# Planned lengths of matrix products, and VectorE planned apart from GpSimd, in a kernel that plans its own queues

## The chip, the cores and the metric

The kernel runs on one core of a Trainium2 chip. The metric is the device time of one execution in microseconds (us). TensorE is called PE here, VectorE DVE, ScalarE ACT, GpSimd POOL and SyncE SP, as in the profile. The clock that TensorE is granted has two levels, 1.2 and 2.4 GHz.

## The reference

Two transformer blocks work on 512 tokens of 1024 features, in float32. The first has a convolution layer and a layer of forgetting attention, each with a feed-forward network and a gated projection of a side input. The second has three branches that are gated and summed, and a gated feed-forward network. Cut to what matters here:

```python
# first block, layer 0 then layer 1
h = h + conformer_conv(rmsnorm(h), ...)         # layer 1: h + fox_attention(...), 16 heads of 64
h = h + square(relu(rmsnorm(h) @ ffn_w1)) @ ffn_w2
h = h + sigmoid(rmsnorm(h) @ ple_w_gate) * (p @ ple_w_proj)
# second block
xa, ga, qm, km, vm, qx, g_logits = split(rms_norm(x) @ w_in)
y_a = rg_lru(causal_dwconv(xa), ...) * gelu(ga)     # gated linear recurrence
y_b = moba_attention(qm, km, vm)                    # 8 heads of 64
y_c = memory_cross_attention(qx, mem_k, mem_v)      # 4 heads of 128
x = x + sum(sigmoid(g_logits) * branch_out(y_a, y_b, y_c)) @ w_out
x = x + (gelu(causal_dwconv(h @ w_gate)) * (h @ w_up)) @ w_down
```

## The kernel before

Activations lie feature-major: a tile holds 128 features by 512 tokens. A product of float32 accuracy is made of three products of float32r halves: weights come as panels of 2048 columns, and each panel is split into `hi` (a cast by ACT) and `lo` (a subtraction by DVE or POOL), each input into `xh` and `xl`; `mm3` issues hi times xh, hi times xl and lo times xh. Most of the program is such groups of 24 products of 512 columns into one bank of PSUM.

Beside this stream run side jobs: the splits of the next panels, the splits of new activations, norms, and the attention heads. A head takes four blocks of 128 queries; for each, PE makes scores (`sc`), DVE the maximum, ACT the exponential `P` (which frees the bank of the scores, of which there are two), POOL scales `P` by the reciprocal, PE transposes it (`ptp`), ACT and DVE split the transposed block (`pth`, `ptl`), and at the end of a head PE multiplies with the values.

No scheduler of a compiler sets the order. The kernel writes instructions in the order in which its own planner reaches them, and each engine runs its own in that order. Every operation goes through `Engine` (line 73): it issues the instruction and asks a cost function (lines 98 to 121) how long it will take. `Flow.account` (line 144) sets the end of the operation on a planned clock: not before the engine's previous one, and not before its inputs. After each operation of PE the planned time moves on and `poll` starts each side job that is then due. `quiet` tells a side job to go on when the named engines are planned to be free. So a duration in a cost function decides how many products stand in the queue of PE before the next step of a side job, and in what order the queues of ACT, DVE and POOL are filled. Nothing is timed at run time: waits are on semaphores.

The planned length of a float32r product is set at line 121:

```python
    return max(0.109 if dt == F32R else 0.059, n / 2390)
```

Three places matter below. In the recurrence of the second block (from line 1328), ACT makes the gelu of four tiles `ga`, after which each is multiplied by the recurrence's output and split (`ya`):

```python
        for f in range(4):
            act.activation(ga[f], ga[f], AF.Gelu_apprx_tanh)
            yield flow.quiet(act)
        for f in range(4):
            yield [ga[f], xc[f]]
            dve.tensor_mul(ga[f], ga[f], xc[f])
            yield ga[f]
            ya[f] = split(ga[f])
```

`branch` (line 1442) multiplies two gate panels (`gl`) with the input and then a panel `br` with `ya`; its first product needs `ya[0]`. The heads of the block attention run beside it. The second place is the end of the forgetting attention (from line 1236): the output panels `("o", 1, 0)` and `("o", 1, 1)` take the last heads' results as they come. The third is a norm (`Front.chain`, line 495): the sum of squares of the last tile goes to PE (`tp<-C,sq`), through DVE and POOL, and back to PE (`tp<-C,s`), beside the 48 products of the first panel of the next stage.

Of the kernel before, what the change touches and what calls it, by code (L numbers as in the profile page):

```python
# [8 lines left out]
F32 = mybir.dt.float32  # L9
F32R = mybir.dt.float32r  # L10
# [5 lines left out]
S = 512  # L16
# [8 lines left out]

# [1 line left out]
_VECS = [  # L27
# [45 lines left out]
class Engine:  # L73
    """an engine whose instructions are issued in the order of the trace, with an estimate of when each one ends"""

    def __init__(self, flow, eng, cost):
        self.flow, self.eng, self.cost, self.t, self.table = flow, eng, cost, 0.0, None

# [36 lines left out]
def _pe_cost(op, out, ins):  # L115
    n, dt = ins[1].free_size(), ins[1].dtype
    if op == "transpose" or (dt == F32 and n == 1):
        return 0.11
    if dt == F32:
        return 0.01 + n * 4 / 2400  # L120
    return max(0.109 if dt == F32R else 0.059, n / 2390)


class Flow:
    """Weaves side work into the stream of matrix products. Every engine issues in the order of this trace; a side is
    a generator that yields what its next step waits for: a time (us), tiles, or a condition."""

# [16 lines left out]
    def account(self, eng, outs, ins, cost):  # L144
        ko = [k for a in outs for k in self.spans(a)]
        ki = [k for a in ins for k in self.spans(a)]
        at = eng.t
        for k in ki + ko:
            at = max(at, self.ready.get(k, 0.0) - (WRITE if k in ko else 0.0))
        for k in ko:  # L150
            at = max(at, self.used.get(k, 0.0))
        eng.t = at + cost
        for k in ki:
            self.used[k] = max(self.used.get(k, 0.0), eng.t)
        for k in ko:
            self.ready[k], self.used[k] = eng.t + WRITE, eng.t
        if eng is self.pe:
            self.now = eng.t
            self.poll()
# [67 lines left out]
def kernel(ctx: ExitStack, tc, gain0, x_t, p_t, mem_t, vec, w, w_f, w_lru, rows, consts, out):  # L227
# [9 lines left out]
    flow = Flow()  # L237
    act, dve = Engine(flow, nc.scalar, _act_cost), Engine(flow, nc.vector, _dve_cost)
    pool, pe = Engine(flow, nc.gpsimd, _pool_cost), Engine(flow, nc.tensor, _pe_cost)
    flow.pe = pe  # L240

# [39 lines left out]

# [1 line left out]
    V = cp.tile([128, NV], F32, name="V")  # L283
# [11 lines left out]

# [1 line left out]
    raws, parts = {}, {}  # L297
# [9 lines left out]
    def part(i, k, pieces, low):  # L307
        """piece k of a panel's split, its low part on engine low"""
        if k == 0:
            parts[i] = tuple(wp.tile([128, PW], F32R, name=nm(n), tag=n, bufs=2) for n in ("hi", "lo"))  # L310
        r, (hi, lo), c = raws[i], parts[i], PW // pieces
        s = slice(c * k, c * k + c)
        gain = GAINED.get(_KEYS[i][0])
        if gain is not None:
            g = col(gain, k)
            act.activation(hi[:, s], r[:, s], AF.Copy, scale=g)
            dve.scalar_tensor_tensor(lo[:, s], r[:, s], g, hi[:, s].bitcast(F32), op0=ALU.mult, op1=ALU.subtract)
        else:
            act.copy(hi[:, s], r[:, s])
            low.tensor_sub(lo[:, s], r[:, s], hi[:, s].bitcast(F32))  # L320
# [40 lines left out]
    def gemm(ps, pan, c0, xs, width=256, ks=None, m=128):  # L361
        """ps += panel columns (from c0 of each k tile)^T x; ks: the k tiles of this call"""
        hi, lo = pan
# [7 lines left out]
    def couter(pan, xs, ks=None, banks=None):  # L371
        """both output tiles of a panel, k tile by k tile"""
        banks = banks or [bank(), bank()]
        for k in range(len(xs)) if ks is None else ks:
            for j in range(2):
                gemm(banks[j], pan, 128 * j, xs, ks=[k])
        return banks

    def pairs(keys, xs):
        """output tiles of the panels in turn; the first panel k tile by k tile, while x still comes"""  # L380
        for i, key in enumerate(keys):
# [9 lines left out]

# [1 line left out]
    def split(src, g=None, n=S, scale=None):  # L393
        """exact two-part float32r split of src * g (g per feature)"""
        xh, xl = slot(F32R, "xh"), slot(F32R, "xl")
# [8 lines left out]
    def split_into(dst, k, src, g=None):  # L404
        """the same in steps, into dst[k]"""
        n = src.shape[-1]
# [12 lines left out]
    class Norm:  # L419
        """per-token mean over features of squares"""  # L420

# [48 lines left out]
    class Front:  # L470
        """input of a stage: gained splits of the stream's tiles as they come, and the norm's factor"""

# [36 lines left out]

# [1 line left out]
    G0 = cp.tile([128, KT], F32, name="G0")  # L511
# [32 lines left out]
    def diagonals(fs):  # L544
        """diagonal matrices of the last PE_TAPS[f] taps of a tile, both parts"""
        for f in fs:
# [27 lines left out]
    def conv_dve(order):  # L574
        """two tiles at a time, tap by tap in turn, so that none waits for its own sum; sums in PSUM"""
        todo, active = list(order), []
# [112 lines left out]

    # products that wait for nothing of the stream: ple projections, memory keys and values  # L690
    prd = dp.tile([KT, 128, S], F32, name="prd")

    def gemm32(ps, raw, c0, xs, width, m=128):
        """float32 products as they are, for panels whose splitting would hold other engines up"""
        n = len(xs)
# [64 lines left out]

    # layer norm over features, two passes
    ys = [None] * KT
# [56 lines left out]

# [1 line left out]
    def squared(z, k, t):  # L821
# [37 lines left out]

# [1 line left out]
    def diag(t, i):  # L861
        """query block i of transposed probabilities: key block j, query block i lies at column 384 j + 128 i"""
        a = t[:, 128 * i:128 * i + 128]
        return bass.AP(tensor=a.tensor, offset=a.offset, ap=[a.ap[0], [384, i + 1], [1, 128]])

    class Head:
        """causal attention of the head in rows 64 half.. of kt() and qt(); out() [128, S] takes a pair of heads"""

# [137 lines left out]
        def weigh(self):  # L1006
            """out[64 rows] = values^T probabilities^T; [V_hi | V_lo] or [V_lo | V_hi]"""
            vs = self.vs()
# [22 lines left out]
    class MemHead(Head):  # L1031
        """attention of one head of 128 features to the memory"""

# [48 lines left out]
    def attend(heads, period, gap):  # L1082
        """scores head by head, at least a period apart; all that follows as its inputs come"""
        state = {"scored": 0}
# [17 lines left out]
    def values(key, xs, r4):  # L1102
        """token-major values of 4 heads, split: per key block [128, 512]"""
        pan = panel(key)
        vs = []
        for b in range(4):
            ps = bank()
            token_major(ps, pan, xs, b)
            t = slot(F32R, "v")
            # heads 0,2: [hi|lo]; heads 1,3: [lo|hi]  # L1110
            v5 = t.rearrange("p (a b c d) -> p a b c d", a=2, b=2, c=2)
# [8 lines left out]

# [1 line left out]
    # the stream's tiles go in as they are, the gains into the weights; h is the sum of the two parts again  # L1122
    xs = front.xs
# [141 lines left out]

# [1 line left out]
    gg = small(8, "gg")  # L1267
# [47 lines left out]

    # gated linear recurrence
    xa, ga = [None] * 4, [None] * 4
# [10 lines left out]
    def recurrence():  # L1328
        # -8 softplus(-lam)
        lam = V[:, _VOFF["lam"]:_VOFF["lam"] + 4]  # L1330
# [53 lines left out]
        for f in range(4):  # L1384
# [4 lines left out]
            yield q  # L1389
            # 1 - a^2 = -tanh(log a) (1 + a^2)  # L1390
            dve.scalar_tensor_tensor(th[f], q, 1.0, th[f], op0=ALU.add, op1=ALU.mult)
# [24 lines left out]

    # block attention: of two blocks of 256 keys the past one is always chosen, so every earlier key counts
    rw, rr_ = slot(p="rows"), slot(F32R, "rowsr")
# [65 lines left out]

    # memory cross attention
    qx = [None] * 4
# [22 lines left out]

    # gated feed forward with a causal convolution on the gate  # L1510
    norms = [Norm(HALF) for _ in range(2)]
# [35 lines left out]

    # the last two panels token half by token half: the first one's norm and output go beside the second's products
    pre = [slot(p="out") for _ in range(2)]
# [67 lines left out]

# [1 line left out]
def _pack(inp):  # L1619
# [3 lines left out]
    def wide(m, c0, n):  # L1623
        """columns c0..c0+n of m [K, N] as [128, K/128 * n]"""
        k = m.shape[0] // 128
# [96 lines left out]

    # shapes alone: identity, causal mask, 1/1024, distance rows
    consts = np.zeros((128, 257), np.float32)
# [41 lines left out]
```

## Time and profile before

| what | value |
|---|---|
| time, median of 3 runs | 2154.78 us (2154.36 to 2157.05) |
| the profiled execution: span, first to last instruction | 2154.4 us (the page gives no other time of its own) |
| PE busy with products | 2109.2 us, 98% of the span, 9920 instructions |
| DVE, ACT, POOL busy | 1270.6, 937.4, 370.5 us |
| mean granted clock of TensorE | 0.993 of 2.4 GHz |
| moved by DMA | 204.79 MB, 95 GB/s on average |

The busy share of PE counts from each product's start to its modelled end, and consecutive products overlap; the pitch from start to start says more than the mean duration. What the table can't say is where PE stands still, and for whom: that is read from the waits, engine by engine, and from the timeline around each.

### The profile page before, as it was taken

What the parts mean: (1) busy time and instruction counts of PE and PEld (TensorE: products, weight loads), DVE (VectorE), ACT (ScalarE), POOL (GpSimd) and SP (SyncE); (2) the same over time, 40 slices, a digit from 0 to 9 for tenths busy, and PEclk for the clock granted to TensorE, in tenths of its full rate; (3) what the DMA queues carried; (4) which work ended last, traced back from release to release, by engine and by line L of the source; (5) the groups of instructions that cost most, each with busy time, mean ns of one, the idle gap of its engine ahead of it and who ended that gap; (6) DMA issues with size and microseconds to landing.
All of it is one profiled execution on the core that took longest, in us unless ns stands there. A gap on an engine that the chain in (4) does not pass through costs nothing. (4 is left out here: it accounts for less than half of the span.)

```text
span 2154.4 us, 26102 instructions
## 1 busy us (share of the span) xinstructions
PE 2109.2 (98%) x9920; PEld 1741.6 (81%) x9920; DVE 1270.6 (59%) x2166; ACT 937.4 (44%) x1884; POOL 370.5 (17%) x380
## 2 busy tenths in 40 slices
PE   7999999999999999999999999999999999999998
PEld 6867888888878887788888887778888888888887
DVE  5997534344576887544343567775564556465563
ACT  5766423233446676433232453665452333232222
POOL 5881100000121336300000031331010010000002
PEclk9999999999999999999999999999999999999999
DMA  5215232232222111222222233112222422222221
GB/s 183 98 45 190 86 110 80 97 104 92 98 80 85 61 61 60 79 98 98 98 93 89 95 125 129 71 64 95 98 79 79 142 93 98 100 96 98 95 101 59
DMA packets 38444, 204.79 MB, mean 95 GB/s; under 512 B 4648, under 2 KB 7976, under 8 KB 15920
## 3 DMA queue, kind: packets, MB, share of 16 engines
q1 hardware_dynamic: 37744, 202.62, 26.8%
q8 instruction: 78, 1.28, 0.2%
q10 hardware_dynamic: 576, 0.52, 0.1%
q14 instruction: 46, 0.38, 0.1%
HBM read 195.45 MB, written 7.68 MB: 94 GB/s over the span
## 5 line engine op out<-in xcount | busy, mean ns | idle before, releaser
L83 PE MATMUL mm<-xh,hi 128*128 128x512 f32 (+1 forms) x2544 | 991.5, 390 | 9.3 <-ACT hi L83 8.4
L83 PE MATMUL mm<-xl,hi 128*128 128x512 f32 (+1 forms) x2544 | 990.5, 389 | 0.0
L83 PE MATMUL mm<-xh,lo 128*128 128x512 f32 (+1 forms) x2544 | 990.0, 389 | 0.2
L83 PEld LDWEIGHTS mm<-xh,hi 128*128 128x128 f32 x2544 | 480.2, 189 | 105.0 <-ACT hi L83 8.4
L83 PEld LDWEIGHTS mm<-xh,lo 128*128 128x128 f32 x2544 | 480.1, 189 | 96.5 <-DVE lo L83 1.5
L83 PEld LDWEIGHTS mm<-xl,hi 128*128 128x128 f32 x2544 | 480.2, 189 | 94.3
L83 ACT CAST hi<-raw 128x512 fp32r<-128x512 f32 x636 | 354.3, 616 | 288.6 <-PE mm L83 268.9
L83 DVE TENSOR_TENSOR lo<-raw,hi 128x512 fp32r<-128x512 f32 x584 | 387.9, 713 | 50.3 <-ACT hi L83 48.8
L83 POOL TENSOR_TENSOR sq<-sq,sq 128x512 f32<-128x512 f32 (+1 forms) x69 | 84.7, 1230 | 1330.0 <-ACT sq L83 1329.4
L83 DVE TENSOR_TENSOR h<-mm,h 128x512 f32<-128x512 f32 (+1 forms) x113 | 75.6, 671 | 279.7 <-PE mm L83 279.6
L83 ACT ACTIVATE z<-z 128x512 f32<-128x512 f32 x64 | 40.4, 631 | 205.3 <-DVE z L83 205.3
L83 DVE SCALAR_TENSOR_TENSOR z<-mm,rbc 128x512 f32<-128x512 f32 x64 | 44.0, 690 | 120.7 <-PE mm L83 120.7
L83 POOL TENSOR_SCALAR P<-P,s 128x128 f32<-128x128 f32 (+2 forms) x112 | 65.3, 588 | 243.6 <-DVE s L83 151.0
L83 DVE TENSOR_TENSOR t<-mm,rbc 128x512 f32<-128x512 f32 x80 | 54.9, 688 | 82.5 <-PE mm L83 78.7
L83 DVE TENSOR_TENSOR xl<-z,xh 128x512 fp32r<-128x512 f32 x64 | 44.3, 693 | 74.7 <-ACT xh L83 74.7
L83 ACT ACTIVATE t<-t 128x512 f32<-128x512 f32 x40 | 25.2, 631 | 128.5 <-DVE t L83 128.4
L83 POOL TENSOR_TENSOR acc<-acc,tap 128x482 f32<-128x482 f32 (+29 forms) x60 | 77.3, 1288 | 13.1 <-ACT tap L83 9.5
L83 DVE SCALAR_TENSOR_TENSOR sc<-u,V,sc 128x511 f32<-128x511 f32 (+21 forms) x116 | 78.9, 732 | 0.5
L83 ACT ACTIVATE xh<-h,V 128x512 fp32r<-128x512 f32 x40 | 28.6, 722 | 112.4 <-DVE h L83 112.4
L83 POOL TENSOR_TENSOR lo<-raw,hi 128x512 fp32r<-128x512 f32 x52 | 69.6, 1363 | 38.8 <-ACT hi L83 38.6
L83 ACT CAST pth<-ptp 128x128 fp32r<-128x128 f32 (+2 forms) x112 | 46.1, 418 | 53.2 <-PE ptp L83 52.6
L83 ACT ACTIVATE P<-sc,s 128x128 f32<-128x128 f32 (+2 forms) x112 | 58.5, 524 | 18.1 <-DVE s L83 17.4
(228 smaller groups left out, 2235.8 us busy)
## 6 DMA issues: line engine op xcount, KB each, us to landing
raw<-in_w SPq DMA_DIRECT2D x175, 1024.0 KB
h<-in_x_t SPq DMA_DIRECT2D x8, 256.0 KB
prd<-pr SPq DMA_DIRECT2D x8, 256.0 KB
pr<-prd SPq DMA_DIRECT2D x8, 256.0 KB
resid<-h SPq DMA_DIRECT2D x8, 256.0 KB
h<-resid SPq DMA_DIRECT2D x8, 256.0 KB
out<-out SPq DMA_DIRECT2D x12, 128.0 KB
raw<-in_w SPq DMA_DIRECT2D x4, 256.0 KB
```

Source lines behind the costliest of these rows:

```text
L83: f(out, *args, **kw)
```

## The change

It alters the planner alone; the computation, its tiles and its pools stay. The planned length of a float32r product of n columns becomes 0.0133 + n/2400 us and at least 0.11 (for 512 columns 0.2267 in place of 0.2142), that of a float32 product at least 0.25 (with one column 0.25 in place of 0.11). DVE operations with two inputs in SBUF of at least 64 elements, and POOL operations with one such input, are planned one after the other: each keeps in `lock` when it ends, and the other engine's next such operation starts no earlier. The costs of ACT, DVE and POOL are as before. The docstrings and comments that the diff also drops are left out here.

```diff
@@ class Engine
-        self.flow, self.eng, self.cost, self.t, self.table = flow, eng, cost, 0.0, None
+        self.flow, self.eng, self.cost, self.t, self.table, self.lock = flow, eng, cost, 0.0, None, 0.0
@@ def _pe_cost(op, out, ins):
     n, dt = ins[1].free_size(), ins[1].dtype
-    if op == "transpose" or (dt == F32 and n == 1):
+    if op == "transpose":
         return 0.11
     if dt == F32:
-        return 0.01 + n * 4 / 2400
-    return max(0.109 if dt == F32R else 0.059, n / 2390)
+        return max(0.25, 0.01 + n * 4 / 2400)
+    return max(0.11, 0.0133 + n / 2400) if dt == F32R else max(0.059, n / 2390)
@@ def account(self, eng, outs, ins, cost):
         at = eng.t
+        other = {self.dve: self.pool, self.pool: self.dve}.get(eng)
+        locks = other is not None and sum(
+            a.space != bass.MemoryType.PSUM and a.free_size() >= 64 for a in ins) >= (2 if eng is self.dve else 1)
+        if locks:
+            at = max(at, other.lock)
...
         eng.t = at + cost
+        if locks:
+            eng.lock = eng.t
@@ def tile_two_blocks_kernel
-    flow.pe = pe
+    flow.pe, flow.dve, flow.pool = pe, dve, pool
```

The queues come out in another order almost everywhere: the operations are the same ones, but for ACT_TABLE_LOAD, which ACT's queue holds 23 times before and 29 times now.

The first place is ACT's queue in the second block, where the four gelus stand (`ga`; `P` is an exponential of an attention block, `hi` a cast of a weight panel). Before:

```order
L83 ACT_TABLE_LOAD
L83 ACTIVATE ga1822_10866<-ga1822_10866 128x512
L83 ACTIVATE ga1823_10868<-ga1823_10868 128x512
L83 ACTIVATE ga1837_10932<-ga1837_10932 128x512
L83 ACTIVATE ga1851_10995<-ga1851_10995 128x512
L83 CAST hi1890_11278<-raw1870_11148 128x512
L83 ACT_TABLE_LOAD
L83 ACTIVATE P1904_11355,s1905_11356<-sc1893_11298,s1898_11317 128x128
L83 ACTIVATE P1906_11363,s1907_11364<-sc1899_11320,s1900_11330 128x256
L83 CAST xh1908_11368<-ga1822_10866 128x512
```

The same place in ACT's queue now, from the third gelu to the fourth (the first two stand 29 and 17 rows earlier):

```order
L83 ACT_TABLE_LOAD
L83 ACTIVATE ga1835_10928<-ga1835_10928 128x512
L83 ACT_TABLE_LOAD
L83 ACTIVATE P1965_11566,s1966_11567<-sc1951_11523,s1952_11530 128x512
L83 CAST pth1960_11552<-ptp1967_11569 128x2x128
L83 COPY t1969_11582<-mm1968_11572 64x512
L83 ACTIVATE P1973_11593,s1974_11594<-sc1962_11556,s1964_11564 128x128
L83 ACT_TABLE_LOAD
L83 ACTIVATE ga1846_10980<-ga1846_10980 128x512
L83 CAST pth1960_11552<-ptp1977_11604 128x3x128
L83 ACT_TABLE_LOAD
```

The four gelus stood in a row behind one table load, ahead of the first exponential; now exponentials stand between them, each change of function loads a table, and the split of `ya[0]` (`xh1994`, a CAST from ga1822) comes seven rows behind the last gelu.

The same place in PE's queue: the last products of the second tile of the first gate panel, and the first product of panel `br`, which takes `ya[0]`. Before:

```order
L83 MATMUL mm1936_11455<-xh1775_10572,hi1890_11278 128x512
L83 MATMUL mm1936_11455<-xl1776_10573,hi1890_11278 128x512
L83 MATMUL mm1936_11455<-xh1775_10572,lo1891_11279 128x512
L83 MATMUL mm1949_11516<-xh1908_11368,hi1922_11416 128x512
L83 MATMUL mm1949_11516<-xl1909_11369,hi1922_11416 128x512
```

Now the last product of the gate panel is followed by side work; these are the first rows of it:

```order
L83 MATMUL mm1926_11420<-xl1776_10604,hi1890_11263 128x512
L83 MATMUL mm1926_11420<-xh1775_10603,lo1891_11264 128x512
L83 MATMUL ptp1941_11491<-C_75,P1923_11415 128x128 x3
L83 MATMUL ptp1944_11499<-C_75,P1928_11432 128x128 x4
L83 MATMUL sc1947_11511<-kk1894_11305,qq1896_11307 128x384
```

and these the last of it, with the first product of panel `br` (`mm1938`):

```order
L83 MATMUL sc1985_11627<-maskb_77,identb_76 128x128
L83 MATMUL sc1989_11640<-kk1953_11532,qq1955_11534 128x128
L83 MATMUL sc1989_11640<-k21954_11533,q21956_11535 128x128
L83 LDWEIGHTS identb_76
L83 MATMUL sc1989_11640<-maskb_77,identb_76 128x128
L83 MATMUL ptp1991_11647<-C_75,P1973_11593 128x128
L83 MATMUL mm1938_11487<-xh1994_11653,hi1910_11377 128x512
```

Where one group of products followed the other, 43 rows of attention work now stand between: seven blocks of scores, 18 transposes and the eight products of one head with the values.

The third place is PE's queue at the norm after the forgetting attention (`tp1417` is the mean of squares, `tp1420` its inverse root spread over the partitions). Before:

```order
L83 MATMUL mm1408_7825<-xh1397_7768,hi1399_7770 128x512
L83 MATMUL tp1417_7881<-C_75,sq1389_7741 128x1 x4
L83 MATMUL mm1408_7825<-xl1398_7769,hi1399_7770 128x512
L83 MATMUL mm1408_7825<-xh1397_7768,lo1400_7771 128x512
```

And now:

```order
L83 MATMUL mm1409_7826<-xh1411_7831,hi1400_7774 128x512
L83 MATMUL tp1417_7898<-C_75,sq1389_7743 128x1 x4
L83 MATMUL mm1409_7826<-xl1412_7832,hi1400_7774 128x512
L83 MATMUL mm1409_7826<-xh1411_7831,lo1401_7775 128x512
L83 MATMUL tp1420_7909<-C_75,s1419_7904 128x128 x4
```

The mean stood behind the first product of the panel's sixth group of inputs and stands now behind the fourth product that takes the last tile; the second `tp` follows two products later, before it was nine.

## Rows read from the trace of the kernel before

**Rows 1.** The page: span, busy time of PE, granted clock in 40 slices.
```profile
span 2154.4 us, 26102 instructions
PE 2109.2 (98%) x9920; PEld 1741.6 (81%) x9920; DVE 1270.6 (59%) x2166; ACT 937.4 (44%) x1884; POOL 370.5 (17%) x380
PEclk9999999999999999999999999999999999999999
```
**Rows 2.** Waits of PE: for whom; us in total, times, longest.
```profile
PE tp L83 <- DVE sq L83: 15.6, 7, 4.7
PE mm L83 <- ACT hi L83: 8.4, 1, 8.4
PE ptp L83 <- DVE ptl L83: 2.6, 1, 2.6
```
**Rows 3.** The chain that ended last: start, us, what.
```profile
1594.91 56.70 PE mm L83 x250
```
**Rows 4.** Windows: stretch, its length, busy PE, PEld, DVE, ACT, POOL, then clock.
```profile
903.80:913.80 10.00, 7.76 (x26) 6.88 (x27) 3.92 (x7) 2.38 (x6) 1.39 (x1) 0.50 0.53 200
```
**Rows 5.** Timeline of ACT at the gelus: start, us, what.
```profile
1389.59 1.28 ACT L83 ACT_TABLE_LOAD   x1
1390.89 2.19 ACT L83 ACTIVATE ga<-ga 128x512 f32<-128x512 f32 x4
```
**Rows 6.** ACT by form, 1376 to 1500 us: busy us, mean ns, idle before.
```profile
L83 ACT CAST hi<-raw 128x512 fp32r<-128x512 f32 x36 | 20.8, 619 | 0.1
L83 ACT ACT_TABLE_LOAD x8 | 10.3, 1283 | 0.1
...
L83 ACT ACTIVATION_READ_ACCUMULATOR P<-sc,s 128x1 f32 x23 | 4.7, 203 | 0.0
...
L83 ACT ACTIVATE P<-sc,s 128x512 f32<-128x512 f32 x5 | 3.5, 699 | 0.0
...
L83 ACT CAST pth<-ptp 128x512 fp32r<-128x512 f32 x5 | 2.9, 587 | 5.4 <-PE ptp L83 5.4
...
L83 ACT ACTIVATE P<-sc,s 128x128 f32<-128x128 f32 x6 | 2.2, 375 | 6.8 <-DVE s L83 6.8
...
L83 ACT CAST pth<-ptp 128x128 fp32r<-128x128 f32 x6 | 1.6, 262 | 2.0 <-PE ptp L83 2.0
```
**Rows 7.** Waits of ACT, 1376 to 1500 us.
```profile
ACT pth L83 <- PE ptp L83: 13.9, 10, 2.6
...
ACT P L83 <- DVE s L83: 8.5, 4, 4.3
```
**Rows 8.** Waits of PE, 1376 to 1500 us.
```profile
PE sc L83 <- DVE qq L83: 1.1, 1, 1.1
PE mm L83 <- ACT xh L83: 0.6, 1, 0.6
```
**Rows 9.** Timeline of PE: one block of 512 scores, to the next product.
```profile
1401.26 0.50 PE L83 MATMUL sc<-kk,qq 128*128 128x512 f32 x1 [0.32 <-ACT P L83]
...
1401.88 0.48 PE L83 MATMUL mm<-xh,hi 128*128 128x512 f32 x1
```
**Rows 10.** Timeline of PE: a head's products with its values, to the next product.
```profile
837.57 0.48 PE L83 MATMUL mm<-pth,v 128*128 128x512 f32 x1
...
838.88 0.73 PE L83 MATMUL mm<-yh,hi 128*128 128x512 f32 x1
```
**Rows 11.** The chain that ended last: four transposes.
```profile
1586.44 0.44 PE ptp L83 x4
```
**Rows 12.** DVE by form, 1376 to 1500 us.
```profile
L83 DVE TENSOR_REDUCE s<-sc 128x1 f32<-128x512 f32 x6 | 4.1, 680 | 0.2
L83 DVE TENSOR_TENSOR sg<-mm,rbc 128x512 f32<-128x512 f32 x5 | 3.4, 679 | 0.0
```
**Rows 13.** Timelines of POOL and DVE: four sums of two SBUF tiles on each.
```profile
829.75 6.36 POOL L83 TENSOR_TENSOR h<-xh,xl 128x512 f32<-128x512 f32 x4
...
830.47 6.20 DVE L83 TENSOR_TENSOR h<-xh,xl 128x512 f32<-128x512 f32 x4
```
**Rows 14.** Timeline of PE at the norm after the forgetting attention.
```profile
900.97 0.39 PE L83 MATMUL mm<-xh,hi 128*128 128x512 f32 x1
906.04 1.86 PE L83 MATMUL tp<-C,sq 128*128 128x1 f32 x8 [4.68 <-DVE sq L83]
```

## The prediction

> **What bounds the kernel now.** I read the page first: PE is busy for 2109.2 of 2154.4 us at the full clock nearly throughout [rows 1]. So the kernel is bound by PE's queue, and a new order of the same instructions can win or lose only where PE stands still. The waits of PE come second: 15.6 us for sums of squares, 2.6 us for one attention tile, and 8.4 us at the start, for the first weights, which no order changes [rows 2]. The chain comes third, for the pitch of a product: 250 of them took 56.70 us, 0.2268 each [rows 3]. The new planned length, 0.2267, is thus the traced one, and the old one, 0.2142, was 5.5% short. Fourth, the windows: behind a wait PE runs at half its clock for a while; the longest such stretch here is 10 us, with PE busy for 7.8 of them [rows 4].
>
> All that can be won is therefore about 18 us of waits [rows 2] and some 7 us of half clock behind them. The price can be any length, because the planner is free to put into PE's queue a run of side work with no product in it, and PE then goes only as fast as ACT, DVE and POOL feed that side work. Old plan and chip differed in a useful way: the planned PE ran ahead of the real one, so side work reached PE's queue later, counted in products, than the chip needed it. The new plan takes that reserve away.
>
> **The change, part by part.**
>
> *The run without products at the first branch.* This is the largest term. The orders in the section on the change show it: 43 rows of attention stand between the last product of the gate panel and the first of panel `br`, which needs the split of `ya[0]`, which ACT issues seven rows behind its fourth gelu. Before, the four gelus took 2.19 us behind one load of 1.28 [rows 5]. From the sigmoid of the last gate product (its input is that product, so it can't start earlier) to the split of `ya[0]`, ACT's queue now holds: 5 table loads at 1.283, 6.4 us; 7 exponentials, two each of 128, 256 and 384 columns and one of 512, between 0.375 and 0.699, 3.6 us; 7 reads of their sums at 0.203, 1.4 us; 7 splits of transposed blocks between 0.262 and 0.587, 3.0 us; and 11 operations of 512 columns at 0.62 (4 `hi`, 2 gelus, 2 head inputs, the sigmoid, a copy, the split itself), 6.8 us [rows 6]. Together 21.2 us. Operations in a row overlap: four gelus took 2.19 where four times 0.62 is 2.48 [rows 5, 6], so each of the 32 that are not loads costs 0.1 less, and the sum is 18.0 us. In front of it stands DVE's evacuation of the gate product, 0.68 us [rows 12].
>
> So at least 18.7 us pass between these two products. PE's own work in between is 18 transposes at 0.11 [rows 11], 2.0 us; eight products with the values, 1.3 us [rows 10]; and seven blocks of scores, two of them of 512 at 0.62 [rows 9], the others taken at half of that or a little more, 2.9 us; 6.2 us in all. PE idles for at least 12.5 us. That is the lower bound, since it lets ACT wait for nothing. For the upper one I let ACT wait as often as it did in this stage before: 13.9 us over 21 splits of transposes and 8.5 us over 23 exponentials [rows 7], which for seven of each is 7.2 us. That makes 12.5 to 19.7 us, and I take 16.0: PE answers faster when no products stand before its transposes, but DVE's part of each round is not shortened.
>
> It takes the place of the wait of 0.6 us for a split of `ga` in the same stage; the wait for the first head's `qq`, 1.1 us, stays [rows 8]. Behind it PE should run at half its clock as behind the other long waits: the stretch in [rows 4] cost half of its 7.8 busy us at most, 3.9, and 2.3 is my value. Sum of this place: 16.0 - 0.6 + 2.3 = 17.7 us. Six more table loads are in ACT's queue in all; ACT is not the bound elsewhere (937.4 of 2154.4 us, [rows 1]), so they cost nothing beyond this place, unless a step of a head stands behind one.
>
> The Trainium skill (ScalarE: Activation LUTs, "What ACT_TABLE_LOAD costs") speaks against loads more strongly: it puts a switch of tables at 1283 ns and about 1380 ns of drain, 2.66 us together. By it the five loads would cost 6.9 us more and the sum below would become 2183.0. The trace of this case does not show the drain: the load ends at 1390.87 and the gelu starts at 1390.89 [rows 5].
>
> *The end of the forgetting attention.* The first products of panel ("o", 1, 0) stood behind the last block of scores before; now nine blocks of scores stand behind the first of them, so fewer products are left to hide the last heads' rounds. A block frees its bank of two after scores, maximum and exponential, 0.62 + 0.68 + 0.70 [rows 6, 9, 12] for the widest, so nine blocks need up to 9 us if nothing else covers them. Transposes and value products of the same heads do cover a good part. Bounds 0 and 9 us, less the wait of 2.6 us that stands there now [rows 2], which may go; I take +4.0, near the middle.
>
> *The norms.* At the norm after the forgetting attention the wait for the sum was 4.7 us [rows 2, 14]. The first `tp` stands 15 products later, but the second only 8 later, and both must be passed: 8 x 0.2268 = 1.8 us won [rows 3]. The same count (8 and 8) holds at the norm after the first feed-forward network; at the norm of the second block it is 2 products, 0.5 us. That is -4.1 us. Against it stands the norm of the memory keys, whose first `tp` moved 17 products forward, up to 3.9 us if its sum does not move as well; I take a quarter, +1.1. Net -3.0 us, bounds -4.1 and 0, and up to 3 us of half clock might go with a shorter wait.
>
> *VectorE apart from GpSimd.* The rule is true to the chip: four sums of two SBUF tiles took DVE 6.20 us beside four on POOL that took 6.36 [rows 13], 1.55 each where DVE needs 0.68 alone [rows 12]. But to plan a delay is not to remove it. Both queues still hold these operations, and with them planned longer the heads are spread out and end later. I price what this and the shorter reserve do at all other places (some hundred waits for panels and blocks, none of which shows today) at +3.0 us, between 0 and 8.
>
> Sum: 17.7 + 4.0 - 3.0 + 3.0 = +21.7 us on the profiled 2154.4, 2176.1. The median of the runs lies 0.4 above that span, so **2176.5 us**. About 0.2%, 4.3 us, is what a measurement of this kernel can tell from no change.
>
> **The rivals.** *Faster: the waits for sums go.* The mechanism is DVE's two-tile operations standing behind POOL's in front of PE; its place is the norms and the attention's end. What it can give is 18.2 us of waits [rows 2] and 7 of half clock; with the run at the first branch at its lower bound, 12.5, the time is 2154.8 - 25.2 + 12.5 = 2142. For it speaks that the planner now knows what stretched those operations [rows 13]. Against it, the order shows only 8 more products at the norm with the longest wait, and part of the 15.6 us is the first and the last norm, which no product can cover. It decides if more than 13 us of waits go. Chance 0.05.
>
> *No change.* The run costs its lower bound and no half clock, the other places cost nothing, norms and half clock return 7: 2154.8 + 11.9 - 4.1 - 2.6 - 3 = 2157. It needs every term at its end. Chance 0.08.
>
> *The plan is starved at more than one place.* ACT waits in the run as before (19.7), PE runs it at half clock, the attention's end costs 9 and the other places 8: 2154.8 + 19.1 + 3.9 + 9 + 8 = 2195 and, with the drain of the loads, beyond 2200. For it speaks that the new plan takes the reserve away everywhere at once. Chance 0.12 for over 2192.
>
> **How the numbers follow.** The forecast has 0.75. Its own range is 2162 to 2192: the run at 12.5 to 19.7 and the other terms inside their bounds. The range that should hold 8 of 10 adds a part of the starved case and a little of the middle ground below: 2160 to 2197. Slower by over 0.2% is the forecast and the starved case, 0.87; within 0.2%, 0.08; faster, 0.05.
>
> **What would show it.** In the profile after, PE must have a stretch of some 19 to 26 us in the stage of the recurrence and the first attention heads that holds no product of a panel, with ACT busy nearly throughout it and table loads between gelus and exponentials; PE's idle time there is 12 us or more, and the windows show half clock behind it. The wait for the sum after the forgetting attention should be shorter than 4.7 us, the busy time of PE's products the same. I am wrong if that stretch is there but ACT's split of `ya[0]` comes within 10 us of the last gate product, or if PE's waits outside it have shrunk by as much as it costs.

## The result and the profile after

| kernel | median of the runs, us | against the kernel before |
|---|---|---|
| before | 2155.32 (2154.36 to 2157.05, 4 runs) | |
| changed | 2182.06 (2179.55 to 2185.66, 4 runs) | 1.0126, 95% interval 1.0114 to 1.0138 |

The change costs 26.7 us; 21.7 were forecast. In the page, PE's busy time rose by 13.0 us to 2122.2 (a product counts for longer at half clock), with the same 9920 instructions, and one slice of 40 shows a granted clock of 0.7 (the lines of before are [rows 1]):

```profile
span 2180.1 us, 26105 instructions
PE 2122.2 (97%) x9920; PEld 1746.6 (80%) x9920; DVE 1271.7 (58%) x2166; ACT 945.4 (43%) x1890; POOL 367.4 (17%) x380
PEclk9999999999999999999999999979999999999999
```

The waits of PE (whom it waited for; us in total, times, longest) changed their kind. The wait for sums of squares fell from 15.6 to 4.4 us [rows 2], and in its place stand many waits for a head's own rounds:

```profile
PE sc L83 <- ACT P L83: 9.8, 11, 2.2
PE mm L83 <- ACT hi L83: 8.0, 1, 8.0
PE ptp L83 <- POOL P L83: 4.5, 4, 2.6
PE tp L83 <- DVE sq L83: 4.4, 3, 2.4
PE tp L83 <- POOL s L83: 3.3, 3, 1.5
PE tp L83 <- POOL acc L83: 3.1, 1, 3.1
```

The slice with the low clock is the first branch. This is the timeline of PE there, first the last product of the gate panel, then waits of the side work, then the first product of panel `br`:

```profile
1415.77 0.40 PE L83 MATMUL mm<-xh,lo 128*128 128x512 f32 x1
1417.08 1.33 PE L83 MATMUL ptp<-C,P 128*128 128x128 f32 x7 [0.92 <-POOL P L83]
1420.66 0.45 PE L83 MATMUL sc<-kk,qq 128*128 128x384 f32 x1 [2.25 <-ACT P L83]
...
1424.88 0.45 PE L83 MATMUL ptp<-C,P 128*128 128x128 f32 x1 [2.64 <-POOL P L83]
...
1438.66 0.79 PE L83 MATMUL mm<-xh,hi 128*128 128x512 f32 x1 [0.87 <-ACT xh L83]
```

22.9 us pass between two products of panels. ACT's timeline in the same stretch shows the sigmoids of the gate panel, then the loads between gelus and exponentials, each followed at once by its operation, and at the end the split of `ya[0]`:

```profile
1416.40 1.28 ACT L83 ACT_TABLE_LOAD   x1
1417.69 1.15 ACT L83 ACTIVATE sg<-sg 128x512 f32<-128x512 f32 x2
...
1426.01 1.28 ACT L83 ACT_TABLE_LOAD   x1
1427.31 0.63 ACT L83 ACTIVATE ga<-ga 128x512 f32<-128x512 f32 x1
1427.95 1.28 ACT L83 ACT_TABLE_LOAD   x1
1429.25 0.69 ACT L83 ACTIVATE P<-sc,s 128x512 f32<-128x512 f32 x1
...
1431.40 1.28 ACT L83 ACT_TABLE_LOAD   x1
1432.69 0.63 ACT L83 ACTIVATE ga<-ga 128x512 f32<-128x512 f32 x1
...
1437.98 0.62 ACT L83 CAST xh<-ga 128x512 fp32r<-128x512 f32 x1
```

And the windows, of this stretch, of the one behind it, and of one in the forgetting attention (stretch, length, busy PE, PEld, DVE, ACT, POOL, then granted clock, share of the DMA engines and GB/s): in the first, ACT is busy for 21.55 of 23.0 us, PE for 13.12 at a mean clock of 0.63.

```profile
1415.70:1438.70 23.00, 13.12 (x51) 8.82 (x49) 13.80 (x37) 21.55 (x42) 6.68 (x11) 0.63 0.26 92
1438.70:1448.00 9.30, 8.17 (x28) 6.33 (x28) 6.11 (x14) 4.27 (x11) 1.04 (x2) 0.64 0.01 2
868.50:875.30 6.80, 6.49 (x18) 4.69 (x19) 4.64 (x9) 3.03 (x10) 6.53 (x8) 0.50 0.00 0
```

**Where the time went.** PE's products other than side work (all but those that write `tp`, `ptp` or `sc`, or read `pth` or `ptl`) are 8836 in every kernel here. So the start of the k-th of them in one trace can be set against its start in the trace of before. The differences, cut into stages at products 900, 2700, 3750, 5250 and 6000 (243, 658, 949, 1291 and 1483 us before), in us:

| kernel | convolution layer | first feed-forward, norm | forgetting attention, its norm | to the second block | its norm, recurrence, first branch | rest | sum |
|---|---|---|---|---|---|---|---|
| changed | +6.2 | -2.0 | +3.9 | +0.1 | +16.0 | +1.4 | +25.7 |
| e1, lengths alone | +15.7 | +1.9 | +2.6 | +0.1 | +9.0 | +0.1 | +29.4 |
| e2, rule alone | +5.0 | -1.4 | +1.5 | 0.0 | +16.5 | -1.0 | +20.6 |
| e3, gelus in a row | +7.0 | -1.9 | +4.1 | +0.1 | +7.6 | +1.6 | +18.4 |
| e4, sums on DVE | -0.1 | +1.5 | -4.6 | 0.0 | -0.9 | 0.0 | -4.1 |
| e5, 0.2205 | +10.3 | +3.5 | +0.5 | +0.1 | +3.0 | +0.2 | +17.6 |
| e6, 0.2048 | +10.6 | -2.3 | -7.3 | -0.2 | +18.1 | +0.7 | +19.6 |
| e7, old in the convolution | +1.1 | -2.0 | +5.5 | +0.1 | +15.9 | +1.6 | +22.2 |
| e8, old from the recurrence on | +6.6 | -2.0 | +4.3 | +0.1 | -0.6 | -0.1 | +8.3 |
| e11, 0.2147 | +6.5 | +2.0 | +0.5 | 0.0 | +5.8 | -0.6 | +14.1 |
| e12, 0.2138 | +10.1 | +1.1 | -0.7 | 0.0 | -0.4 | -2.1 | +8.0 |
| e9, by stages | +1.1 | -2.0 | -3.7 | 0.0 | -0.2 | -0.1 | -4.9 |
| e10, by stages, sums on DVE | +1.2 | -2.0 | -6.2 | 0.0 | -0.5 | -0.1 | -7.5 |

Each row compares one profiled execution with one, and the first weights alone vary by about 1 us, so a difference of a few tenths means little, one of two us in one cell does.

### The profile page after: what moved, and what is told of

The parts are those of the page before. It is cut to its first block, busy times and chain, and to the rows that moved or that the text cites. A ratio compares the mean times of both kernels' runs of the same rounds, so it can differ in the third digit from the quotient of the medians.

```text
span 2180.1 us, 26105 instructions
## 1 busy us (share of the span) xinstructions
PE 2122.2 (97%) x9920; PEld 1746.6 (80%) x9920; DVE 1271.7 (58%) x2166; ACT 945.4 (43%) x1890; POOL 367.4 (17%) x380
## 3 DMA queue, kind: packets, MB, share of 16 engines
q8 instruction: 78, 1.28, 0.2%
## 5 line engine op out<-in xcount | busy, mean ns | idle before, releaser
L83 DVE SCALAR_TENSOR_TENSOR sc<-u,V,sc 128x494 f32<-128x494 f32 (+28 forms) x116 | 78.7, 733 | 0.5
L83 ACT ACTIVATE P<-sc,s 128x128 f32<-128x128 f32 (+2 forms) x112 | 58.2, 522 | 22.9 <-DVE s L83 21.3
```

The source lines that it names most:

```text
L83: f(out, *args, **kw)
```

## The experiments

**Which half of the change.** e1 keeps the lengths and drops the rule:

```diff
         locks = other is not None and sum(
...
-        if locks:
-            at = max(at, other.lock)
```

> The new planned lengths of products, without the rule that keeps DVE and POOL apart. In its order the longest run of side work in PE's queue is 27 rows at the end of the forgetting attention, as before the change, and 19 rows in the first branch, where the changed kernel has 47 rows. The theory (the price is the run without products at the first branch, and it comes with the rule): the 17 us of that place do not appear, PE idles less than 3 us there, and the time is 2154 to 2166 us (2155 plus the convolution stage's 6 at most plus up to 5 at other places). The rival (the lengths alone take the planned reserve away, as the prediction put it, and with it the time): 2172 us or more, lost at many places of 0.5 to 2 us.

Measured: 2184.85 us, ratio 1.0130 (1.0115 to 1.0145), as slow as the whole change. The theory's time missed by 19 us, though its place was right: there is no run at the first branch. The rival was right on the time, not on the places: instead of many losses of 0.5 to 2 us, two stages lose 24.7 of the 29.4. The waits of PE are mostly those of before, longer ([rows 2] for 15.6 and 8.4; the third line stood at 1.1 in [rows 8]):

```profile
PE tp L83 <- DVE sq L83: 20.5, 7, 6.0
PE mm L83 <- ACT hi L83: 11.9, 3, 7.3
PE sc L83 <- DVE qq L83: 4.4, 1, 4.4
PE ptp L83 <- DVE s L83: 4.0, 4, 2.8
```

e2 keeps the rule and takes the old lengths back:

```diff
-    if op == "transpose":
+    if op == "transpose" or (dt == F32 and n == 1):
         return 0.11
     if dt == F32:
-        return max(0.25, 0.01 + n * 4 / 2400)
-    return max(0.11, 0.0133 + n / 2400) if dt == F32R else max(0.059, n / 2390)
+        return 0.01 + n * 4 / 2400
+    return max(0.109 if dt == F32R else 0.059, n / 2390)
```

> The rule that keeps DVE and POOL apart, with the old planned lengths of products. Its order has a run of 53 side rows at the first branch (47 in the changed kernel). The theory (the rule makes the run, the run makes the time): 19 to 26 us between the last gate product and the first product of the branch panel, half clock behind it, and a time of 2170 to 2188 us. The rival (the shorter reserve of the lengths is what costs): PE with the old lengths still runs ahead of the chip, so the rounds of the heads are covered, and the time is 2165 us or less.

Measured: 2177.70 us, 1.0097 (1.0082 to 1.0112), as the theory had it. 25.4 us pass between the gate product and the next one; over them ACT is busy for 23.72 us and the granted clock is 0.65:

```profile
1408.30:1433.70 25.40, 13.99 (x56) 9.52 (x54) 15.29 (x38) 23.72 (x45) 5.47 (x10) 0.65 0.23 83
```

So of these two halves the rule alone makes the run at the first branch, and the lengths alone lose mostly by longer waits; e6 below makes the run without either. They don't add: 29.4 and 20.6 alone, 25.7 together. In the convolution layer the lengths alone lose 15.7 us, the lengths with the rule 6.2. e1 holds both new lengths, that of float32r and that of float32 products; no run takes them apart.

**The gelus.** e3 is the changed kernel without the pause between them:

```diff
             act.activation(ga[f], ga[f], AF.Gelu_apprx_tanh)
-            yield flow.quiet(act)
```

> The changed kernel with its four gelus issued in a row, nothing else altered. In its order the split of ya[0] stands ahead of the sigmoids of the gate panel, and there are no 47 side rows before the first product of the branch panel. The theory (five table loads and the heads' work between the gelus hold the branch up): the stretch without products shrinks from 22.9 us to under 6, the half clock behind it goes, and the time falls by 13 to 20 us, to 2162 to 2169 us. The rival (the heads' own rounds over ACT, DVE and POOL are what PE waits for, and they only move elsewhere): the time falls by less than 6 us, to 2176 us or more, with new waits for P and ptp in the stage.

Measured: 2174.97 us, 1.0082 (1.0065 to 1.0099), 7.1 us less than the changed kernel. That lies between the two forecasts, and the other stages are within 0.8 us of the changed kernel's. The run is gone: the longest stretch without such a product in this stage is under 4 us. But PE now waits for one split of `ya` after the other (its waits over the whole kernel; the changed kernel's own two lines of this kind are 2.7 and 2.1):

```profile
PE mm L83 <- ACT xh L83: 5.4, 4, 2.7
...
PE mm L83 <- DVE xl L83: 3.7, 3, 1.8
```

ACT's timeline shows what holds them up: the gelus end at 1411.3, yet the four splits are spread over 13 us, behind exponentials, a load for the sigmoids and the multiplications on DVE (three of the four splits are shown):

```profile
1409.12 2.19 ACT L83 ACTIVATE ga<-ga 128x512 f32<-128x512 f32 x4
...
1416.86 0.63 ACT L83 CAST xh<-ga 128x512 fp32r<-128x512 f32 x1
1417.51 1.28 ACT L83 ACT_TABLE_LOAD   x1
...
1422.32 0.60 ACT L83 CAST xh<-ga 128x512 fp32r<-128x512 f32 x1
...
1430.01 0.62 ACT L83 CAST xh<-ga 128x512 fp32r<-128x512 f32 x1 [0.84 <-DVE ga L83]
```

About half of the price of the place (16.0 against 7.6) is thus the pauses between the gelus; the other half stays, and this timeline puts it to the heads' work and the loads that are still ahead of the splits.

**The sums.** e4 is the kernel before with one constant changed:

```diff
-H_POOL = (1, 3, 5, 7)
+H_POOL = ()
```

> The kernel before, with all eight sums of two SBUF tiles of h at the forgetting attention's entry on DVE instead of four on DVE and four on POOL. The theory (DVE and POOL exclude each other in such operations, so the four on POOL win nothing): the eight sums take 5.4 to 5.9 us on DVE alone (0.68 each), not longer than the 6.2 to 6.4 us of four beside four, and the time is within 3 us of the kernel before. The rival (each side is only slowed, and the pair still ends sooner than one engine would): the eight take 7 us or more and the norm behind them starts later, 2158 us or more.

Measured: 2151.90 us, 0.9984 (0.9974 to 0.9993), faster than before by 2.7, within what the theory allowed. DVE alone makes all eight in less time than four beside four took [rows 13]:

```profile
831.84 5.31 DVE L83 TENSOR_TENSOR h<-xh,xl 128x512 f32<-128x512 f32 x8
```

The wait of 2.6 us for `ptl` behind them [rows 2] is not in this trace.

**More or less reserve.** e5, e6, e11 and e12 are the kernel before with one number changed (2322, 2500, 2385, 2395):

```diff
-    return max(0.109 if dt == F32R else 0.059, n / 2390)
+    return max(0.109 if dt == F32R else 0.059, n / 2322)
```

> The kernel before with the planned length of a float32r product halfway between the old and the new one (0.2205 us for 512 columns), no rule for DVE and POOL. The theory (each per cent of planned reserve taken away makes PE wait longer at the same places): about half of what the full length cost alone, 2165 to 2174 us. The rival (the length only decides, by jumps, which of several orders the planner picks, and the lengths-alone kernel got a bad one): not in between, so under 2160 or over 2179 us.

> The kernel before with a still shorter planned length (0.2048 us for 512 columns), so that the plan has more reserve than before; no rule for DVE and POOL. Its order has, although nothing of the rule is in it, a run of 56 side rows at the first branch. Theory of the reserve alone: all side work reaches PE later than it is ready, and the time is 2158 us or less. Theory of the run (it costs wherever it comes from): 17 to 24 us at the first branch, little at other places, 2168 to 2180 us.

Measured: 2174.15 us for e5, 1.0091 (1.0073 to 1.0109), and 2176.20 for e6, 1.0099 (1.0083 to 1.0114). e5 alone looks like the smooth theory, 0.15 us over its upper end. e6 contradicts it: with more reserve than before, the convolution layer loses 10.6 us too. That e6's time lies in the range of the theory of the run is in part luck, for little was to be lost elsewhere: the 10.6 us are nearly balanced by 9.6 won in the next two stages. At the first branch e6 has the run without any rule, and it costs 18.1 us: loads between gelus and exponentials on ACT, and the split of `ya[0]` 26 us behind the first of the sigmoids:

```profile
1406.59 1.23 ACT L83 ACTIVATE sg<-sg 128x512 f32<-128x512 f32 x2
1407.83 1.28 ACT L83 ACT_TABLE_LOAD   x1
...
1418.01 1.28 ACT L83 ACT_TABLE_LOAD   x1
1419.30 0.63 ACT L83 ACTIVATE ga<-ga 128x512 f32<-128x512 f32 x1
1419.95 1.28 ACT L83 ACT_TABLE_LOAD   x1
...
1432.61 0.62 ACT L83 CAST xh<-ga 128x512 fp32r<-128x512 f32 x1
```

So the run costs wherever it comes from, and neither part of the change is needed for it. The smooth theory was then tried with 0.2% up and down:

> The kernel before with the planned length of a product 0.2% longer (0.2147 us for 512 columns), nothing else. If the time follows the reserve smoothly (17.6 us lost for 3% at 0.2205): 0 to 2 us, so 2154 to 2157 us. If each length draws another order, and the old one is a good draw that the kernel's other constants fit: a loss of 4 to 15 us at one or two places, 2158 us or more.

> The same 0.2% shorter (0.2138 us). Smooth reserve: 2153 to 2156 us. Drawn orders: 2158 us or more, lost at one or two places, and not at the places of the 0.2% longer one.

Measured: 2169.36 us for e11, 1.0068 (1.0054 to 1.0081), and 2162.93 for e12, 1.0034 (1.0021 to 1.0048). Less than half a nanosecond in the planned length of a product (0.45 of 214.2 ns) costs 14 us in one direction and 8 in the other. The forecast of drawn orders holds for the times, and only in part for the places: only e11 loses at the recurrence (5.8), but both lose most in the convolution layer (6.5 and 10.1). The time does not follow the reserve.

**Stage by stage.** e7 and e8 are the changed kernel with a switch that gives `_pe_cost` the old lengths and `account` no rule, e7 up to the first feed-forward network, e8 from the recurrence on:

```diff
+    if PLAN["old"]:
+        if op == "transpose" or (dt == F32 and n == 1):
+            return 0.11
...
-        locks = other is not None and sum(
+        locks = not PLAN["old"] and other is not None and sum(
...
+    PLAN["old"] = True
     flow.spawn(recurrence())
```

> The changed kernel with the old lengths and without the rule up to the end of the convolution layer; both are in force from the first feed-forward network on. The order behind that point has the same long runs (50, 47 and 39 side rows) as the changed kernel. If the price is made stage by stage: the 6.2 us of the convolution stage go, the rest stays, 2174 to 2178 us. If the stages hang together (the plan of a later stage shifts with that of an earlier one): anywhere else, under 2172 or over 2180 us.

> The changed kernel with the old lengths and without the rule from the start of the recurrence of the second block on. In its order the run of 47 side rows at the first branch is gone. If the run is what costs there: the 16.9 us of that stage go and nothing else does, 2163 to 2168 us. If the heads' rounds are what PE waits for, with or without the run: new waits for P, ptl and xh in the same stage and 2172 us or more.

Measured: 2178.20 us for e7, 1.0109 (1.0091 to 1.0127), 0.2 us over the upper end of the first forecast; by stages 5.1 us of the convolution layer's 6.2 are gone (e9 and e10, which plan that layer as before too, have the same 1.1 left), the second block pays the same 15.9, and the forgetting attention 1.6 more. e8: 2163.98 us, 1.0042 (1.0027 to 1.0058), as forecast; the whole 16 us of the first branch go and nothing takes their place. The waits of PE from 1300 to 1500 us in the changed kernel begin with

```profile
PE sc L83 <- ACT P L83: 5.3, 5, 2.2
PE ptp L83 <- POOL P L83: 4.1, 3, 2.6
```

and in e8 with

```profile
PE mm L86 <- DVE xl L86: 1.8, 1, 1.8
PE sc L86 <- ACT xh L86: 1.6, 1, 1.6
PE sc L86 <- DVE xl L86: 1.4, 2, 1.2
```

**A plan of the best stages.** e9 uses the switch with a length: old up to the first gated projection, lengths and rule of the change for that projection and its norm, 0.2048 without the rule for the forgetting attention, old again behind it. e10 adds the `H_POOL` of e4.

```diff
+    PLAN["per_us"] = None
     ple(0, pf, pr, lambda f: front.add(f, h[f]))
...
     xs = front.xs
+    PLAN["per_us"] = 2500
...
+    PLAN["per_us"] = 2390
     ffn(1, nf, pf)
```

> A plan made of the best stages seen: the old planner up to the first gated projection, the changed one (both lengths and rule) for that projection and its norm, a short length (0.2048 us, no rule) for the forgetting attention, and the old planner from the second feed-forward network on. If the stages add up as measured in their own runs: 0 in the convolution, -2 at the norm, -4 to -7 in the forgetting attention, 0 behind it, so 2145 to 2150 us. If the order of a stage hangs on what was planned ahead of it: a draw like the others, 2158 us or more.

> The plan by stages with all eight sums of two SBUF tiles on DVE. If both gains add up: 2142 to 2148 us. If the sums gave their 2.7 us only by the order that they happened to draw in the forgetting attention, they give nothing here or cost: 2148 us or more, not below the plan by stages alone.

Measured: e9 2147.25 us, 0.9969 (0.9957 to 0.9980); e10 2149.88, 0.9971 (0.9960 to 0.9983). e9 beats both kernels, the one before by 0.20 to 0.43%. Its traced execution took 2151.33 us, more than the median, so the stages show 4.9 us where the medians differ by 8.0. What the stage of the forgetting attention gives, 3.7, can be seen in the timeline of the norm behind it, where the wait of 4.68 [rows 14] became 2.37, and in the wait for `ptl`, 2.6 [rows 2] and now 0.9 from 690 to 920 us; the first norm gives 2.0, and the convolution layer, planned as before, stands at +1.1 all the same:

```profile
902.22 1.72 PE L86 MATMUL tp<-C,sq 128*128 128x1 f32 x8 [2.37 <-DVE sq L86]
```

e10 shows a further 2.5 us in that stage of its one trace, but its runs are not faster than e9's: whether the sums add anything there stays open.

## Why the prediction was right, and where not

**The time** lies in the range, 5.6 us over the forecast, and the forecast case, slower, came true. By places: the norm behind the first feed-forward network -1.8 predicted and -2.0 measured, the forgetting attention with its norm +2.2 and +3.9, the second block's norm and first branch +17.2 and +16.0, all the rest +4.1 and +7.7.

**The run at the first branch: right in sum, wrong in its parts.** +17.7 was predicted, and the stage pays 16.0, in which the second block's norm gains 1.0 (0.5 was predicted), so that 17.0 fall to the branch. The stretch was to be 16.0 of idle and 6.2 of work, 22.2 together; it is 22.9. ACT is busy nearly throughout, as the sum of its queue had it (18.0 and 0.68 were the floor). The 3.5 us by which the prediction went over its floor were to be waits of ACT, though, and ACT idles for only 1.45 of the 23.0. They went elsewhere: the last sigmoid starts at about 1418.2, 2.5 us behind the start of the last gate product where 0.68 was counted, since DVE comes to that product only at 1417.07 and ACT has the end of a gelu and a load in front; and from there to the end of the split 20.4 us pass where 18.0 were summed, 1.2 of them a wait for a transposed block. That the sum came out so near is thus in part luck. And PE was to idle for 12 us or more and idles for 23.0 - 13.1 = 9.9: the half clock came inside the stretch, not only behind it, so the 6.2 us of side work count as 13.1 busy us, and much of what was counted as idle is work at half clock. The rest is the tail of each separate group, which a sum by pitch leaves out: the first 7 transposes took 1.33 us, still at full clock, where 7 times 0.11 is 0.77. For the same reasons PE's busy time, which was to stay the same, rose by 13.0 us. Behind the stretch the half clock lasts until 1445.3, another 6.6 us, worth up to 3.3 where 2.3 was taken:

```profile
1421.50:1445.30 23.80, 17.21 (x60) 12.81 (x59) 15.19 (x35) 19.17 (x39) 5.42 (x9) 0.50 0.13 45
```

The loads cost what [rows 5] said: the next operation starts 0.01 to 0.02 us behind each (1426.01 + 1.28 and 1427.31). The Trainium skill (ScalarE: Activation LUTs, "What ACT_TABLE_LOAD costs") adds some 1380 ns of drain to each; no trace here shows it.

**Norms, and the forgetting attention: right, with one sum a little off.** A quarter of the 3.9 us at the memory keys is 1.0, not the 1.1 that was taken. The norm behind the first feed-forward network gained 2.0 where 1.8 was predicted. Attention and its norm together cost 3.9, where +4.0 and -1.8 made 2.2. The wait of 4.68 at that norm is gone:

```profile
920.39 0.95 PE L83 MATMUL tp<-C,sq 128*128 128x1 f32 x8
```

The heads' waits in front of it (0.2 to 1.5 us each) take more than that back: PE's waits in this stage are 10.7 us where they were 8.2, and 4.5 of them are six waits of scores for the exponential that frees their bank, the mechanism that was predicted. What makes up the rest of the 3.9 was not taken apart. Some of these waits are followed by half clock: in the window from 868.50 PE is busy for 6.49 of 6.80 us at 0.50.

**All other places: too small, and at a place that was not named.** +3.0 there and +1.1 for the memory keys were predicted; the convolution layer took 6.2 and the rest 1.4. The largest wait of that layer, but for the start, is not at the memory keys, where the wait fell from 1.25 to 0.43 us, but at the layer norm, 3.1 us for the convolution's sums (`tp <- POOL acc`, 1.4 before) with half clock behind it; a wait of 1.6 for a DMA of weights is new. The prediction had looked at the orders of the attention and of the norms, and in that layer at the memory keys alone.

**The cause: the step that failed is "the new plan takes that reserve away".** Three results speak against it as the explanation. A length with more reserve than before (e6) loses as much as one with less (e5). A change of 0.2% in either direction loses 8 to 14 us. And the run at the first branch, for which the prediction, reading it from the order, names no other reason than the shorter reserve, comes with the rule alone (e2), doesn't come with the full new length alone (e1), and comes with a shorter length (e6). What the runs show in its place: every new number in the planner draws another order, stage by stage, and all five other lengths tried were worse over the whole program than the old one. That the kernel's other planned times (delays, periods, slacks) were chosen under the old numbers and no longer fit is the likely reason, but it is only argued: no run sets them anew under the new lengths.

**VectorE apart from GpSimd.** For sums of this kind the rule is true, as [rows 13] said, and e4 shows it in another way: eight sums on DVE end sooner than four and four. The Trainium skill says the same (SBUF — State Buffer, "Who interferes with whom": the two engines share one pair of ports under an exclusive lock, and a VectorE instruction with two inputs in SBUF contends for it with a GpSimd instruction that reads SBUF). The trace agrees, 5.31 against 6.20 and 6.36 us. But only e4, which moves the work off POOL, removes the collision. With the rule planned, the eight sums still overlap on the chip in the changed kernel and take 7.24 us from the first start to the last end, where they took 6.91 before. Planning around the collision with the old lengths (e2) won no more than 1.4 us at any stage, at the first norm.

## What to carry to other kernels

Truer durations in a planner do not by themselves make a better plan: look at the order that it draws, above all for runs of side work in the bound engine's queue, and price each by the queue of the engine that feeds it. Before a loss is put down to a mechanism, vary the number by a fraction of a per cent both ways; if that alone moves the time by a good part of the effect (here 0.2% by 14 and 8 us, where the full new lengths moved it by 30), the number selects among orders and its direction explains little. Where the stages turn out nearly independent, the best plan can be put together stage by stage. Where two engines hold each other up, as in the sums here, try giving the work to one of them; e4 won 2.7 us by it, while e10, on top of the plan by stages, was not faster in its runs.

## What the runs showed of the hardware

Short waits close together were followed by the half clock, and it went on while PE was nearly always busy: from 864 to 869 us of the changed kernel PE waited three times, 0.72, 0.34 and 1.49 us, and from 868.5 to 875.3 it ran at 0.50 while busy for 95% of the time.

```profile
864.88 0.50 PE L83 MATMUL sc<-kk,qq 128*128 128x512 f32 x1 [0.72 <-ACT P L83]
...
866.33 0.50 PE L83 MATMUL mm<-yh,hi 128*128 128x512 f32 x1 [0.34 <-ACT yh L83]
...
868.75 0.79 PE L83 MATMUL mm<-yl,hi 128*128 128x512 f32 x1 [1.49 <-DVE yl L83]
```

In the trace of before the half clock at the norm came with a single long wait, the 4.68 us that end at 906.04 [rows 4, 14]; with the waits of e9 (2.37 us in place of 4.68 at the same norm) a window of 6.75 us there has the half clock, and behind 909.3 it is full again, where before it lasted some 10 us:

```profile
902.45:909.20 6.75, 6.75 (x23) 5.78 (x23) 1.67 (x4) 0.00 (x0) 1.40 (x1) 0.50 0.48 159
...
909.30:911.00 1.70, 1.70 (x11) 1.44 (x11) 0.43 (x1) 0.59 (x1) 0.00 (x0) 1.00 0.00 0
```
